# Eight DRAM-to-DRAM copies of 384-column bias lines in place of eight broadcast stores of 160-column pieces

## The chip, the core and the metric

The kernel runs on one core of one Trainium2 chip. The metric is the device time of one execution in microseconds (us); the time of a kernel is the median of its runs. A profiled execution gives in addition the span from its first to its last instruction, and what each engine, the queue of SP and the DMA engines did in it.

## The reference, cut to what matters

A decoder layer on 2048 tokens plus 16 meta tokens: RMSNorm, one input projection to 1952 columns, three token mixers side by side (latent attention with 6 heads, differential attention with 4 heads, sliding-window attention with 6 heads), an output projection, a SwiGLU feed forward, and a last norm. Heads of the second and third mixer add a relative position bias, which depends on the distance of query and key alone:

```
n = max(q_pos - k_pos, 0)
bucket = n if n < 16 else min(16 + int(log(n / 16) / log(128 / 16) * 16), 31)
logits = q . k * scale + rel_bias[bucket, head]      # 10 heads with a bias
```

All distances from 128 on share the last bucket. So a head's bias is one line over the distance, and a tile of 128 queries by some keys is that line, read one place further along from query to query.

## The kernel before, in words

The work has four phases on one core: phase A (norm, input projection, latent projections, all results to DRAM), phase B (full attention of latent and differential heads), the window attention with the output projection, and the feed forward.

**Phase A** (line 186) goes over 17 tiles of tokens, `t` = 0 to 16: tile 0 holds the meta tokens, the others 128 tokens each. A tile projects its tokens in four chunks of columns (`project`, matmuls at lines 122 to 124), splits the results into a high and a low half on ACT and DVE (`hilo`, lines 299 and 300), transposes them on PE (`flush`, line 346), copies the transposes out of PSUM (lines 350 and 352) and stores them to DRAM (lines 355 to 372). In the middle of tile `t` the tokens of tile `t + 1` are squared for the norm (ACT, line 325) and transposed (PE, line 332). The tokens themselves are loaded by line 213 into the two buffers of `xt`. The results for V go to a tile `vs` with one buffer, stored by line 475 to `vd`.

**The bias lines** are made beside this. `bias_lines` (line 257) is a generator; the loop of tiles advances it by one step in each tile from `t` = 4 on:

```
if t >= 4:
    next(lines, None)
```

A step loads a piece of a one-hot table (`hot`, line 271), multiplies it with the bias table on PE (line 273), copies the product to SBUF (line 275) and stores it into `ld` in DRAM (line 276) 128 times over, once for each partition, by a source that is repeated:

```
w = LINE // 4                                # 160 columns
...
nc.sync.dma_start(out=ld[r0:r0 + m, :, c:c + w],
                  in_=line[0:m, 0:w].unsqueeze(1).to_broadcast([m, P, w]))
```

There are 17 lines, 11 in the first group (`m` = 11) and 6 in the second, of `LINE` = 640 columns in four pieces each: eight steps, hence the tiles 4 to 11. `ld` is laid out `[17, 128, 640]`: line, partition, column. Each run that a store writes is 160 columns of 4 bytes long.

**Who reads `ld`.** `skew` (line 149) reads it with a step of one element less than a row from partition to partition, so that each partition gets the line one place further on. Phase B does it twice at its start (`ncaus`, lines 531 and 532), the window attention three times (`nswa`, lines 850 to 852).

**What sets the order.** All transfers are issued by SP, in one queue, in the order of a scheduler that works through the whole program with a timeline of its own. On each engine it places an instruction as soon as, on that timeline, what the instruction needs is there; so a load that needs nothing can stand far ahead of its place in the text of the program. What the scheduler has put in order is issued in that order.

Of the kernel before, what the change touches and what calls it, by code (L numbers as in the profile page):

```python
# [10 lines left out]
F32 = mybir.dt.float32  # L11
# [6 lines left out]
DRAM = bass.MemoryType.DRAM  # L18

P = 128  # L20
# [9 lines left out]
NB = 32  # L30
# [4 lines left out]
LINE = 640  # L35
# [12 lines left out]
# input projection: columns grouped as they are multiplied  # L48
# [7 lines left out]
# stacks, all [128, tokens] with high and low halves of float32 side by side  # L56
# [7 lines left out]
def constants():  # L64
    ident = np.eye(P, dtype=np.float32)
    fold = np.concatenate([np.eye(64), np.eye(64)]).astype(np.float32)
    inv = (10000.0 ** (-np.arange(0, 32, 2, dtype=np.float32) / np.float32(32))).astype(np.float32)
    pos = np.zeros((NT + 1, P), np.float32)
    pos[0, :META] = np.arange(META)
    pos[1:] = META + np.arange(SEQ).reshape(NT, P)  # L70
    ang = (pos[:, :, None] * inv).astype(np.float64)
    c, s = np.cos(ang), np.sin(ang)
    rope = np.concatenate([c, c, -s, s], -1).astype(np.float32).transpose(1, 0, 2)
    dist = 511 - np.arange(LINE)
    n = np.maximum(dist, 0)
    big = 16 + (np.log(np.maximum(n, 16) / 16.0) / math.log(DMAX / 16) * 16).astype(np.int64)
    bucket = np.where(n < 16, n, np.minimum(big, NB - 1))
    hot = np.zeros((2, NB + 1, LINE), np.float32)
    hot[:, bucket, np.arange(LINE)] = 1.0
    off = dist < 0  # L80
    far = off | (dist >= DMAX)
    for j, m in enumerate((off, far)):
        hot[j][:, m] = 0.0
        hot[j][NB, m] = 1.0
    return {"c_ident": ident, "c_fold": fold, "c_rope": np.ascontiguousarray(rope),
            "c_hot": np.ascontiguousarray(hot.transpose(1, 0, 2))}


def key_chunks(m):
    # 16 meta keys and m blocks of 128, in chunks of at most CH columns, and each in pieces of at most PW: (first column, width)  # L90
    out, c = [], 0
    for b in ([m] if m <= 8 else [-(-m // 2), m // 2]):
        w = b * P + (0 if c else META)
        n = -(-w // PW)
        pieces = []
        for j in range(n):
            k = (b // n + (1 if j >= n - b % n else 0)) * P + (0 if c else META)
            pieces.append((c, k))
            c += k
        out.append(pieces)  # L100
    return out
# [3 lines left out]
def trunk(ctx: ExitStack, tc: tile.TileContext, a, out):  # L105
# [13 lines left out]
    ld = dram.tile([NLINE, P, LINE], F32, name="ld")  # L119
# [9 lines left out]
    # ------------------------------------------------------------ constants  # L129
# [19 lines left out]
    def skew(dst, row, n, c0, w):  # L149
        # dst [P, n, w]: n lines, each one place further to the left from partition to partition  # L150
        src = bass.AP(tensor=ld.tensor, offset=ld.offset + row * P * LINE + 127 + c0, ap=[[LINE - 1, P], [P * LINE, n], [1, w]])
        nc.sync.dma_start(out=dst, in_=src)

    def merge_to(dst, x, y):
        # two lists of items side by side, in proportion to their costs
        tx, ty = sum(c for c, _ in x) or 1.0, sum(c for c, _ in y) or 1.0
        ix = iy = 0
        ax = ay = 0.0
        while ix < len(x) or iy < len(y):
            if iy >= len(y) or (ix < len(x) and ax / tx <= ay / ty):  # L160
                dst.append(x[ix])
                ax += x[ix][0]
                ix += 1
            else:
                dst.append(y[iy])
                ay += y[iy][0]
                iy += 1

    def rows_of(items):
        # items up to each one without cost, as one  # L170
# [14 lines left out]
    # ------------------------------------------------------------ phase A  # L185
    def phase_a():
        with ExitStack() as st:
            # the weights that the last tile needs first are at the edge, where phase B begins
# [68 lines left out]
            def bias_lines():  # L257
                # relative bias lines (negated, relative to the last bucket) and masks
# [7 lines left out]
                w = LINE // 4  # L266
                for j in range(2):
                    r0, m, b0 = ((0, 11, 0), (11, 6, 4))[j]
                    for c in range(0, LINE, w):
                        hot = stage.tile([P, SW], F32, name="raw")  # L270
                        nc.sync.dma_start(out=hot[0:NB + 1, 0:w], in_=a["c_hot"][:, j, c:c + w])
                        ps = psT.tile([P, 512], F32, name="psT")
                        nc.tensor.matmul(out=ps[0:m, 0:w], lhsT=rb[:, b0:b0 + m], rhs=hot[0:NB + 1, 0:w], start=True, stop=True)
                        line = stage.tile([P, SW], F32, name="raw")
                        nc.vector.tensor_copy(out=line[0:m, 0:w], in_=ps[0:m, 0:w])
                        nc.sync.dma_start(out=ld[r0:r0 + m, :, c:c + w], in_=line[0:m, 0:w].unsqueeze(1).to_broadcast([m, P, w]))
                        yield
# [24 lines left out]
            def rotate(dst, src, t, n):  # L302
                # src, dst: [P, n, 32]
# [36 lines left out]
            def flush(t, src, b, m):  # L340
                # transposed stacks b..b+m to DRAM
# [43 lines left out]
            for t in range(NT + 1):  # L385
# [10 lines left out]
                # [dk dv]  # L396
# [9 lines left out]
                # [c_kv k_rope sk sv]  # L406
# [23 lines left out]
                if not meta:  # L430
                    # [c_q dq]
# [10 lines left out]
                    # [sq]  # L442
# [10 lines left out]
                # latent projections  # L453
# [55 lines left out]
    # ------------------------------------------------------------ phase B  # L509
    def phase_b(window):  # L510
        with ExitStack() as st:
            # on the right what the last products with V no longer need
# [18 lines left out]
            skew(ncaus[:, 4:5, 256:], 10, 1, 256, 256)  # L531
            skew(ncaus[:, 0:4, 256:], 0, 4, 256, 256)
            # P^T of a pair's last key tile: the earlier query tile does not see it
# [6 lines left out]
            def softmax_row(items, i, mm_fn, cost, bias, fin):  # L540
                # items: the logits (negated) piece by piece of keys, with the maximum so far, then the row's
                # exponentials; fin(exponentials, row sum)
# [52 lines left out]
            def pv_pair(items, g, rows, v, fin):  # L595
                # O^T [high|low of v, 256 queries] of one head, then y = both halves, queries first
# [66 lines left out]
            def key_cols(q):  # L663
                # columns that the pairs 2q and 2q + 1 add
                return slice(0 if q == 0 else META + 512 * q, META + 512 * (q + 1))

            def order(h, last):
                # pairs of query tiles of a head; the last heads end with little
                return FORD if h == 0 else LORD if h == last else MORD

            def early(h, q):
                # only the first loads go ahead of the last stores of phase A
# [165 lines left out]
    # ------------------------------------------------------------ window attention, output projection  # L838
    def swa_setup(st):
# [10 lines left out]
        skew(nswa[:, 0, :, 0:16], 4, SH, 368, 16)  # L850
        skew(nswa[:, 0, :, 144:272], 11, SH, 384, 128)
        skew(nswa[:, 1, :, 16:272], 11, SH, 256, 256)
        return sw, sms, snk, nswa

    def phase_o(feed):
        with ExitStack() as st:
# [118 lines left out]
            # the half of w_out that is needed first  # L975
# [8 lines left out]
            # shared with the feed forward  # L984
            wk = shared.enter_context(tc.tile_pool(name="wk2", bufs=2, reuse_waits="tile"))
            common["wk"] = wk
            # what the last products no longer need is closed first
# [31 lines left out]
            def out_items(t):  # L1019
# [46 lines left out]
                def operands(r):  # L1066
                    # what this tile gives to the seven right operands of its chunk (see phase_f)
# [66 lines left out]
    # ------------------------------------------------------------ feed forward  # L1134
    def phase_f():
        # one level of Strassen's products: gate and up over halves of (features, d_model, tokens of a chunk),
        # down over halves of (tokens of a chunk, features, d_model)
        TH, FH = 512, NF // 2
        with ExitStack() as st:
# [16 lines left out]
            # gate and up, right operands: blocks x0, y0 (d_model halves of the first tokens) and x, y (of the second):  # L1156
            # x0 + y, x0, x - y, y0 - x0, y, x + x0, y0 + y
            # left operands: (first block, second block, sign); blocks are numbered 2 * feature half + d_model half
            WS = ((0, 3, 1), (2, 3, 1), (0, None, 1), (3, None, 1), (0, 1, 1), (2, 0, -1), (1, 3, -1))
            XORD = (0, 3, 4, 2, 6, 1, 5)  # L1160
            # down, left operands: blocks of h, numbered 2 * feature half + token half
            HS = ((0, 3, 1), (1, 3, 1), (0, None, 1), (3, None, 1), (0, 2, 1), (1, 0, -1), (2, 3, -1))
            # down, right operands: blocks of w_down, numbered 2 * feature half + column half
            DS = ((0, 3, 1), (0, None, 1), (1, 3, -1), (2, 0, -1), (3, None, 1), (0, 1, 1), (2, 3, 1))
            # (token half, column half, sign) of the sums that a product enters
# [4 lines left out]
            def gate_up():  # L1170
                with ExitStack() as s2:
                    # on the right what begins before the output projection has ended
# [9 lines left out]
                    def operand(c, i):  # L1182
                        # a right operand, split where it is
# [17 lines left out]
                    def weight(blk, i):  # L1201
                        # a left operand
# [21 lines left out]
                    def product(c, blk, close, after):  # L1224
                        # four blocks [128 features, 512 tokens], (feature half, token half), to close()
# [63 lines left out]
                    for n, (c, f, u) in enumerate(steps):  # L1289
# [5 lines left out]
                        def give(i):  # L1295
                            # what this block gives to the left operands of down
# [35 lines left out]
            def start_down():  # L1332
                # what begins before the last product of gate and up has ended
# [31 lines left out]
            def finish_down():  # L1365
                split_right, load_right, left, wsr, bwa, w0, x0 = (down[k] for k in ("split_right", "load_right", "left", "wsr", "bwa", "w0", "x0"))
                with ExitStack() as s2:
# [8 lines left out]
                    def raw(b, f):  # L1376
                        # a block of w_down; the blocks on the diagonal stay
# [57 lines left out]
                    def update(c, i, j, ps):  # L1435
                        # a finished product of token tile j of a half, into the sums
# [75 lines left out]
```

## Time and profile before

| | us |
|---|---|
| time, median of 3 runs | 2902.93 |
| time, lowest and highest | 2899.53, 2908.26 |
| span of the profiled execution | 2904.6 |
| PE busy in it | 2746.6 (95%) |
| DVE, ACT, POOL busy | 1795.9, 1447.5, 1318.6 |

The time of the profiled execution is not given apart from its span; the span lies among the three times. In the profile, PE is TensorE, PEld its weight loads, DVE, ACT and POOL are VectorE, ScalarE and GpSimd, SPq is the queue of SyncE, from which the transfers are issued. A duration on SPq is the time that one issue takes there, not that of its transfer. `PEclk` is the granted clock of TensorE as a share of its upper level of 2.4 GHz (0.50 is the lower level, 1.2 GHz), and `DMA share` the mean busy share of the core's 16 DMA engines. In a wait, the engine and line that waited stand left of the arrow and what it waited for stands right of it.

### The profile page before, as it was taken

The page shows a single profiled execution, that of the slowest core. Times are in us where ns is not written, and L with a number is a line of the kernel's source. Part 1 is how long each engine was busy: PE and PEld are TensorE (multiplying, and loading weights), DVE is VectorE, ACT ScalarE, POOL GpSimd, SP SyncE. Part 2 cuts the span into 40 slices and gives each one's busy share as a digit, 9 for nine tenths or more (in the row PEclk, how much of TensorE's full clock was granted, in tenths as well). Part 3 has the DMA queues.
Part 4 walks back from the last instruction along what each step waited for, and adds up shares of the span by engine and source line. Part 5 has one row for each costly group of instructions (what it writes and reads, how often), then busy time and mean ns, then how long its engine had stood idle before and what let it go on. Part 6 is the DMA issues. An engine that isn't in the chain of part 4 may idle for free.

```text
span 2904.6 us, 44635 instructions
## 1 busy us (share of the span) xinstructions
PE 2746.6 (95%) x14767; PEld 2357.7 (81%) x14767; DVE 1795.9 (62%) x4098; ACT 1447.5 (50%) x3264; POOL 1318.6 (45%) x1585
## 2 busy tenths in 40 slices
PE   7977779999999999989999899999999999999999
PEld 6866668888898999878888688888788888788887
DVE  6322223389898888855545866666866666565564
ACT  6433334478887888864443433334433334343343
POOL 1211112268788788831213555554655554232241
PEclk9988889999999999999999999999999999999999
DMA  7555444684556444366665633324423332944564
GB/s 195 140 125 122 108 113 138 170 236 110 148 120 157 109 122 98 83 196 185 191 184 184 211 106 109 105 89 163 141 95 109 109 98 89 322 133 135 169 194 145
DMA packets 427250, 417.80 MB, mean 144 GB/s; under 512 B 56415, under 2 KB 318202, under 8 KB 425226
## 3 DMA queue, kind: packets, MB, share of 16 engines
q1 hardware_dynamic: 427018, 414.94, 49.7%
q8 instruction: 117, 1.92, 0.3%
q14 instruction: 115, 0.94, 0.1%
HBM read 275.45 MB, written 139.39 MB: 143 GB/s over the span
## 4 chain that ended last, share of the span: by engine, by line
PE 79%; DMA 7%; DVE 4%; issue 4%; SPq 2%; ACT 2%; POOL 2%; POOLq 0%; ACTq 0%; DVEq 0%
PE ps L1221 9%; PE ps L1220 9%; PE ps L1219 9%; PE psO L638 5%; PE psTb L608 4%; PE ps L122 4%; PE ps L123 4%; PE ps L124 4%; PE psA L122 4%; PE psA L123 4%; PE psA L124 4%; PE psS L798 2%; PE psAo L122 2%; PE psAo L124 2%; PE psAo L123 2%
## 5 line engine op out<-in xcount | busy, mean ns | idle before, releaser
L1220 PE MATMUL ps<-x,wgh 128*128 128x512 f32 x1232 | 485.2, 394 | 6.2 <-DVE x L1189 6.1
L1221 PE MATMUL ps<-x,wgl 128*128 128x512 f32 x1232 | 484.9, 394 | 2.2 <-DVE wgl L1211 2.2
L1219 PE MATMUL ps<-x,wgh 128*128 128x512 f32 x1232 | 483.3, 393 | 3.8 <-ACT x L1188 3.8
L1151 POOL TENSOR_TENSOR wsum<-r 128x512 f32<-128x512 f32 x220 | 322.6, 1471 | 333.4 <-DVE wgl L1211 332.0
L575 ACT ACTIVATE p<-p,mn 128x656 f32<-128x656 f32 (+8 forms) x336 | 305.4, 915 | 32.4 <-DVE mn L570 31.4
L1210 ACT CAST wgh<-wsum 128x512 fp32r<-128x512 f32 x220 | 136.3, 620 | 313.8 <-PE ps L1220 205.8
L1220 PEld LDWEIGHTS ps<-x,wgh 128*128 128x128 f32 x1232 | 231.9, 188 | 63.4 <-DVE x L1189 10.7
L1219 PEld LDWEIGHTS ps<-x,wgh 128*128 128x128 f32 x1232 | 232.2, 188 | 57.8 <-ACT x L1188 5.3
L1221 PEld LDWEIGHTS ps<-x,wgl 128*128 128x128 f32 x1232 | 232.0, 188 | 53.7 <-DVE wgl L1211 2.6
L122 PE MATMUL ps<-bh,wgh 128*128 128x512 f32 x616 | 241.5, 395 | 3.2 <-ACT wgh L1356 3.2
L123 PE MATMUL ps<-bl,wgh 128*128 128x512 f32 x616 | 243.2, 395 | 0.0
L124 PE MATMUL ps<-bh,wgl 128*128 128x512 f32 x616 | 238.3, 393 | 0.0
L1211 DVE TENSOR_TENSOR wgl<-wsum,wgh 128x512 fp32r<-128x512 f32 x220 | 189.7, 863 | 58.8 <-ACT wgh L1210 57.8
L608 PE MATMUL psTb<-ident,p 128*128 128x128 f32 x1440 | 218.6, 277 | 2.8 <-DVE ptl L620 1.4
L122 PE MATMUL psA<-wi,xh 128*128 128x512 f32 (+2 forms) x528 | 207.9, 394 | 6.0 <-ACT wi L237 4.8
L123 PE MATMUL psA<-wi,xh 128*128 128x512 f32 (+2 forms) x528 | 202.6, 384 | 0.3 <-DVE wi L238 0.3
L1356 ACT CAST wgh<-wgl 128x512 fp32r<-128x512 f32 x154 | 95.0, 620 | 214.4 <-DMA wgl<-fd 170.1
L124 PE MATMUL psA<-wi,xl 128*128 128x512 f32 (+2 forms) x528 | 201.0, 381 | 0.0
L1357 DVE TENSOR_TENSOR wgl<-wgl,wgh 128x512 fp32r<-128x512 f32 x154 | 117.8, 774 | 131.3 <-ACT wgh L1356 124.8
L638 PE MATMUL psO<-pth,vt 128*128 128x256 f32 x720 | 192.6, 288 | 2.3 <-ACT p L575 2.0
L638 PE MATMUL psO<-ptl,vt 128*128 128x256 f32 x720 | 192.9, 296 | 0.8 <-DVE ptl L620 0.2
L1151 POOL TENSOR_TENSOR hs<-c 128x512 f32<-128x512 f32 x108 | 157.1, 1461 | 55.1 <-DVE c L1310 49.0
(255 smaller groups left out, 6862.7 us busy)
## 6 DMA issues: line engine op xcount, KB each, us to landing
wgl<-fd SPq DMA_DIRECT2D x154, 256.0 KB
fd<-hs SPq DMA_DIRECT2D x110, 256.0 KB
qm<-qd SPq DMA_DIRECT2D x92, 256.0 KB
r<-in_w_gate_dram SPq DMA_DIRECT2D x88, 256.0 KB
r<-in_w_up_dram SPq DMA_DIRECT2D x88, 256.0 KB
ws<-in_w_down_dram SPq DMA_DIRECT2D x77, 256.0 KB
qd<-so SPq DMA_DIRECT2D x80, 192.0 KB
qf<-qd SPq DMA_DIRECT2D x60, 256.0 KB
```

The costliest lines, as they stand in the source:

```text
L122: nc.tensor.matmul(out=ps, lhsT=xh, rhs=wh, start=start, stop=False)
L123: nc.tensor.matmul(out=ps, lhsT=xh, rhs=wl, start=False, stop=False)
L124: nc.tensor.matmul(out=ps, lhsT=xl, rhs=wh, start=False, stop=stop)
L575: nc.scalar.activation(out=x[:, 0:m], in_=x[:, 0:m], func=AF.Exp, bias=mn[:, n:n + 1], scale=-1.0, accum_out=rsum[:, k:k + 1])
L608: nc.tensor.transpose(pt[:, j * 256 + q * P:j * 256 + (q + 1) * P], cols(rows[q], c), ident)
L638: nc.tensor.matmul(out=ot[:, 0:256], lhsT=v[:, vb], rhs=x, start=(st_["n"] == 1), stop=(st_["n"] == 2 * total))
L1151: eng.tensor_tensor(out=out, in0=x, in1=y, op=ALU.add if sign > 0 else ALU.subtract)
L1210: nc.scalar.copy(out=h, in_=src)
L1211: nc.vector.tensor_tensor(out=l, in0=src, in1=f32(h), op=ALU.subtract)
L1219: nc.tensor.matmul(out=ps, lhsT=h[:, k], rhs=o[:, 0, k], start=k == 0, stop=False)
L1220: nc.tensor.matmul(out=ps, lhsT=h[:, k], rhs=o[:, 1, k], start=False, stop=False)
L1221: nc.tensor.matmul(out=ps, lhsT=l[:, k], rhs=o[:, 0, k], start=False, stop=k == 3)
```

## The change

Lines have 384 columns instead of 640 (distances 255 to -128 instead of 511 to -128; the skewed reads start 256 columns earlier, so that they read the same values). A group's line is made in one step, of 384 columns, and stored once, into a small DRAM tile `l1` `[17, 384]`. Eight further steps copy `l1` to `ld`, which is now laid out `[128, 17, 384]`: each copies all 17 lines, 26,112 bytes in one piece, for 16 partitions. The generator so has ten steps instead of eight: two that make lines and eight that copy, in the tiles 4 to 13. The diff, without edits of comments:

```
-LINE = 640
+LINE = 384
...
-    dist = 511 - np.arange(LINE)
+    dist = 255 - np.arange(LINE)
...
-    ld = dram.tile([NLINE, P, LINE], F32, name="ld")
+    l1 = dram.tile([NLINE, LINE], F32, name="l1")
+    ld = dram.tile([P, NLINE, LINE], F32, name="ld")
...
     def skew(dst, row, n, c0, w):
-        src = bass.AP(tensor=ld.tensor, offset=ld.offset + row * P * LINE + 127 + c0, ap=[[LINE - 1, P], [P * LINE, n], [1, w]])
+        src = bass.AP(tensor=ld.tensor, offset=ld.offset + row * LINE + 127 + c0, ap=[[NLINE * LINE - 1, P], [LINE, n], [1, w]])
...
-                w = LINE // 4
                 for j in range(2):
                     r0, m, b0 = ((0, 11, 0), (11, 6, 4))[j]
-                    for c in range(0, LINE, w):
-                        hot = stage.tile([P, SW], F32, name="raw")
-                        nc.sync.dma_start(out=hot[0:NB + 1, 0:w], in_=a["c_hot"][:, j, c:c + w])
-                        ps = psT.tile([P, 512], F32, name="psT")
-                        nc.tensor.matmul(out=ps[0:m, 0:w], lhsT=rb[:, b0:b0 + m], rhs=hot[0:NB + 1, 0:w], start=True, stop=True)
-                        line = stage.tile([P, SW], F32, name="raw")
-                        nc.vector.tensor_copy(out=line[0:m, 0:w], in_=ps[0:m, 0:w])
-                        nc.sync.dma_start(out=ld[r0:r0 + m, :, c:c + w], in_=line[0:m, 0:w].unsqueeze(1).to_broadcast([m, P, w]))
-                        yield
+                    hot = stage.tile([P, SW], F32, name="raw")
+                    nc.sync.dma_start(out=hot[0:NB + 1, 0:LINE], in_=a["c_hot"][:, j])
+                    ps = psT.tile([P, 512], F32, name="psT")
+                    nc.tensor.matmul(out=ps[0:m, 0:LINE], lhsT=rb[:, b0:b0 + m], rhs=hot[0:NB + 1, 0:LINE], start=True, stop=True)
+                    line = stage.tile([P, SW], F32, name="raw")
+                    nc.vector.tensor_copy(out=line[0:m, 0:LINE], in_=ps[0:m, 0:LINE])
+                    nc.sync.dma_start(out=l1[r0:r0 + m], in_=line[0:m, 0:LINE])
+                    yield
+
+                for b in range(0, P, 16):
+                    nc.sync.dma_start(out=ld[b:b + 16].rearrange("p n c -> p (n c)"),
+                                      in_=l1.rearrange("(o n) c -> o (n c)", o=1).to_broadcast([16, NLINE * LINE]))
+                    yield
...
-            skew(ncaus[:, 4:5, 256:], 10, 1, 256, 256)
-            skew(ncaus[:, 0:4, 256:], 0, 4, 256, 256)
+            skew(ncaus[:, 4:5, 256:], 10, 1, 0, 256)
+            skew(ncaus[:, 0:4, 256:], 0, 4, 0, 256)
...
-        skew(nswa[:, 0, :, 0:16], 4, SH, 368, 16)
-        skew(nswa[:, 0, :, 144:272], 11, SH, 384, 128)
-        skew(nswa[:, 1, :, 16:272], 11, SH, 256, 256)
+        skew(nswa[:, 0, :, 0:16], 4, SH, 112, 16)
+        skew(nswa[:, 0, :, 144:272], 11, SH, 128, 128)
+        skew(nswa[:, 1, :, 16:272], 11, SH, 0, 256)
```

## Rows read from the trace of the kernel before

**Rows 1.** The page: TensorE's granted clock in 40 equal slices of the span.

```profile
PEclk9988889999999999999999999999999999999999
```

**Rows 2.** Chain that ended last: start us, us, what; the transposes that bound tiles.

```profile
55.88 0.90 PE psT L332 x8
...
141.34 0.90 PE psT L332 x8
...
452.86 0.87 PE psT L332 x8
...
536.69 0.87 PE psT L332 x8
```

**Rows 3.** Busy time by stretch of phase A: three tiles, eight tiles, three tiles.

```profile
core 0: us, PE busy (x) PEld busy (x) DVE busy (x) ACT busy (x) POOL busy (x), PEclk, DMA share, GB/s
55.90:141.30 85.40, 84.34 (x498) 75.89 (x497) 31.99 (x75) 39.18 (x111) 18.56 (x50) 1.00 0.51 141
141.30:452.90 311.60, 240.81 (x1303) 213.88 (x1302) 88.60 (x204) 101.45 (x284) 47.06 (x129) 0.86 0.50 117
452.90:536.70 83.80, 82.21 (x487) 74.03 (x486) 31.39 (x73) 37.36 (x105) 17.30 (x48) 1.00 0.47 131
```

**Rows 4.** PE's wait in 141.3 to 452.9: total us, times, longest us.

```profile
PE psT L346 <- DVE gm L300: 68.9, 12, 10.1
```

**Rows 5.** ACT's wait for tokens, in 141.3 to 452.9, then in 452.9 to 536.7.

```profile
ACT sq L325 <- DMA xt<-in_x_dram: 102.8, 8, 14.5
...
ACT sq L325 <- DMA xt<-in_x_dram: 0.9, 2, 0.5
```

**Rows 6.** SP's queue in a tile of the first three: start us, us, issue.

```profile
113.34 0.43 SPq L368 DMA_DIRECT2D wd<-so  x1
113.82 0.46 SPq L372 DMA_DIRECT2D wd<-so  x1
114.71 0.35 SPq L213 DMA_DIRECT2D xt<-in_x_dram  x1
```

**Rows 7.** SP's queue in the tile after it, with a step of the lines.

```profile
138.57 0.96 SPq L276 DMA_DIRECT2D ld<-raw  x1
139.57 4.15 SPq L271 DMA_DIRECT2D raw<-in_c_hot_dram  x1
144.16 2.91 SPq L359 DMA_DIRECT2D kd<-so  x1
147.13 3.27 SPq L368 DMA_DIRECT2D wd<-so  x1
150.46 3.02 SPq L372 DMA_DIRECT2D wd<-so  x1
153.59 0.54 SPq L213 DMA_DIRECT2D xt<-in_x_dram  x1
```

**Rows 8.** Busy time by stretch behind a store of 11 lines, then of 6.

```profile
142.00:150.00 8.00, 8.00 (x47) 6.96 (x46) 2.59 (x5) 2.51 (x6) 0.00 (x0) 1.00 0.61 77
...
299.00:307.00 8.00, 8.00 (x45) 6.96 (x44) 2.63 (x6) 2.34 (x6) 0.00 (x0) 1.00 0.33 49
```

**Rows 9.** Busy time by stretch inside the tile that begins at 141.3.

```profile
155.00:160.00 5.00, 0.00 (x0) 0.00 (x0) 0.00 (x0) 1.03 (x2) 0.00 (x0) 0.79 0.77 208
160.00:165.00 5.00, 2.94 (x14) 2.62 (x14) 3.50 (x10) 3.91 (x14) 0.73 (x2) 0.50 0.39 107
```

**Rows 10.** ACT in a tile of the first three; idle before it, and for what, in brackets.

```profile
118.37 1.06 ACT L325 ACTIVATE sq<-xt 128x1024 bf16<-128x1024 f32 x1 [0.60 <-DMA xt<-in_x_dram]
...
122.86 0.48 ACT L352 COPY so<-psT 128x384 f32<-128x384 f32 x1 [3.03 <-PE psT L346]
...
133.04 0.47 ACT L299 ACTIVATE vs<-psA,rs 128x256 fp32r<-128x256 f32 x1 [4.83 <-DMA vd<-vs]
```

**Rows 11.** Chain that ended last: the two passes of a line's matmul.

```profile
137.09 0.37 PE psT L273 x2
```

**Rows 12.** SP's queue near the start: a load that `bias_lines` issues.

```profile
14.60 0.42 SPq L263 DMA_DIRECT2D rb<-in_rel_bias_dram  x1
```

**Rows 13.** Busy time of the stretch with the highest DMA rate looked at, in the feed forward.

```profile
2500.00:2520.00 20.00, 16.77 (x65) 12.90 (x64) 12.04 (x17) 5.50 (x9) 4.16 (x3) 0.91 1.04 396
```

**Rows 14.** Instructions on the skewed tile of phase B: ns min/median/max, first and last start us.

```profile
L570 DVE CUSTOM_DVE_ANT_0 p<-psS,ncaus x42: 297/434/575, 578.7 to 1137.6; 128x400 f32<-128x400 f32 x14, 128x144 f32<-128x144 f32 x14, 128x272 f32<-128x272 f32 x14
...
L152 SPq DMA_DIRECT2D ncaus<-ld x2: 448/458/467, 538.2 to 538.7; - x2
```

## The prediction

> **What bounds the kernel now.** I read the page first. Its row of the granted clock is full but for slices 2 to 5, some 145 to 436 us [rows 1]; that is phase A, and the steps of the bias lines run there. Next the chain that ended last: it passes through the token transposes of every tile, so their starts bound the tiles [rows 2]. Then busy time by stretch between those edges [rows 3]. Three tiles before the steps take 85.4 us and three after them 83.8, so a tile without a step takes 169.2 / 6 = 28.2 us, with PE busy for 166.55 / 6 = 27.76 of it and the clock at 1.00. The eight tiles behind a step take 311.6 us, 38.95 each. PE is idle for 311.6 - 240.8 = 70.8 us of that, and its busy time is 240.8 instead of 8 x 27.76 = 222.1.
>
> The waits say why. PE's idle time is its wait for the halves that ACT and DVE make [rows 4], and ACT, which works in order, had been standing at the squares of the next tokens: 102.8 us in eight waits for their load, against 0.9 in two waits in the three tiles after the steps [rows 5]. The load is late because it is issued late. In a tile without a step SP issues `wd`, `wd` and the tokens at under half a microsecond each [rows 6]; behind the store to `ld` the one-hot load, `kd` and the two `wd` take 2.9 to 4.2 us each, and the tokens go out 153.59 - 138.57 = 15.0 us behind that store [rows 7]. All of these small transfers stand behind the store in one queue. In the eight microseconds behind a store of 11 lines the DMA engines are busy at 0.61 and move 77 GB/s; behind one of 6 lines, 0.33 and 49 GB/s [rows 8]. The first store is 11 x 128 x 640 B = 901 KB, 11.7 us at 77 GB/s; the second is 492 KB, 10.0 us at 49 GB/s. A store of nearly half the bytes thus holds the queue almost as long. A shape in which each line keeps one DMA engine busy explains it: 11/16 = 0.69 and 6/16 = 0.38, near the shares.
>
> The Trainium skill states such a rule (DMA: Bandwidth & Descriptors, Why a DMA increments its semaphore by 16 and not by 1): a copy runs on the largest number of engines up to 16 that divides the outermost counts on both sides. The shares of [rows 8] agree; by it a copy with 16 outermost would have 16 engines.
>
> The gap is paid twice. After PE's idle 155 to 160 us the granted clock is 0.50, 1.2 GHz, in the next 5 us [rows 9]; this is most of the 240.8 - 222.1 = 18.7 us by which PE is busy longer.
>
> **The change, part by part.**
>
> *Eight broadcast stores go.* With them go the late tokens, ACT's stand, PE's idle time and the lower clock behind it: 311.6 - 8 x 28.2 = **-86.0 us**. What is late next in such a tile is seen in the six without a step: nothing; PE is busy for 27.76 of 28.2 us, so PE's own work is the next bound.
>
> *Two lines of 384 columns instead of eight pieces of 160.* The two passes of a piece take 0.37 us on PE [rows 11]; of 384 columns 0.37 x 384 / 160 = 0.89. The eight old ones are already inside the 311.6 us, the six reference tiles hold none, so two new ones on a PE that is full cost **+1.8 us**. The two PSUM copies and two stores to `l1` (17 rows of 1,536 B, 26 KB together) lie beside PE's work; DVE is busy for 32 of 85 us [rows 3].
>
> *Eight copies of 16 x 26,112 B = 417.8 KB.* The trace has no DRAM-to-DRAM transfer, so I bound one from both sides. Below: at the highest rate looked at, 396 GB/s [rows 13], 417.8 KB take 1.06 us. Above: at the rate of one engine in the slowest store, 77 / 11 = 7.0 GB/s [rows 8], one engine's 26,112 B take 3.7 us. Long runs on all engines speak for the low end, a read and a write of DRAM at once and one source for all engines for the high end; I take 2.0 us, the geometric middle. No gain is possible here; the copies are added work.
>
> The same page (Latency and other measured facts) gives 207 GB/s for copies between HBM tensors, and 103 where rows lie a large power of two apart, which speaks against such copies; estimates from it are 2.0 and 4.1 us a copy. With 4.1 us and all eight ahead of the tokens the sum below would end some 3 us above its upper bound. No run here shows it yet.
>
> *Where they are issued.* In the program the copies stand one per tile, in the tiles 6 to 13. But a copy needs nothing except the two stores to `l1`, and the scheduler does not hold back what needs nothing: the load of the bias table, which `bias_lines` issues in tile 4, was issued at 14.6 us [rows 12]. So I expect most of the eight right behind the second store to `l1`, in one burst in tiles 5 and 6, at some 165 to 185 us. The first copy adds a wait on SP for that store to land. Behind it in the queue stand `kd`, `wd`, `wd` and the tokens, and ACT's squares wait for the tokens.
>
> A burst occupies all engines for 8 x 1.06 = 8.5 to 8 x 3.7 = 30 us. What covers it: ACT stands idle 3.03 us behind the squares anyway [rows 10], and the engines are idle for half of a tile, 14 us (share 0.51 [rows 3]). Lower end: every copy falls behind the tokens and into idle engine time, 0 us. Upper end: all eight are ahead of the tokens, 30 - 3 = 27 us, and some 4 us for a PE at the lower clock: 31. I take half of them ahead of the tokens: 4 x 2.0 = 8, less 3 of cover, and 1 for the clock: **+6 us**. Were this cover gone, the tokens would be late by the whole 8. The store of `vs` comes next: ACT waits 4.83 us for it in a tile without a step, and PE does not stop [rows 10], so it has some slack too.
>
> *The skewed reads* keep number, bytes and length of runs; only the steps between runs differ. Those of phase B are issued 40 us before their first use [rows 14], and a burst of copies ends some 250 us ahead of them: 0, with both bounds inside that cover. Those of the window attention come after the whole of phase B and are taken as unchanged.
>
> The sum is 2904.6 - 86.0 + 1.8 + 6 = 2826.4 on the span of the profiled execution. That span is 1.7 us above the median of the runs, so I forecast **2825 us**. The bounds of the burst make it 2819 to 2850.
>
> **The rivals.**
>
> *One copy per tile.* If the copies stay in their tiles, each delays the tokens by at most 3.7 us against 3 of cover, 8 x 0 to 8 x 0.7: 2819 to 2825. For it: the stores went out at their places; against: they had to wait for a product of their tile, and the copies have none. The time is hardly another, but the picture is.
>
> *Copies far dearer than the nearest rows.* Sixteen engines read the same 26 KB at the same moment, and no row shows what this does. At twice the upper bound, 7.4 us, the burst is 59 us and all of it shows but the cover, 3: 2904.6 - 86.0 + 1.8 + 60 = 2880, or 2879 against the median. Still faster.
>
> *A copy that runs on one engine* (the other side). If the lowering puts the whole repeated source on one ring, that engine moves 417.8 KB a copy. At 396 / 16 = 24.8 GB/s this is 16.8 us, 135 for eight, and every transfer with a share on that ring waits: 2904.6 - 86.0 + 1.8 + 135 - 3 = 2952, less 1.7: about 2951. It decides from 84 + 3 = 87 us for all eight, 11 us a copy. Against it stands that 11 and 6 outermost lines kept about that many engines busy [rows 8], so 16 should keep 16.
>
> *Late tokens in every tile with a step, whatever it moves.* Then ten steps instead of eight stall, 86.0 / 8 = 10.75 us each: 2903 + 21.5 = 2924. Against it: 901 KB and 492 KB moved the stall little, but by the same runs per engine, which a copy does not have. If only a part of the mechanism holds, the result could also land at no change.
>
> **How the numbers follow.** My forecast with a burst, within 2819 to 2850, has 0.62; one copy per tile 0.20; dearer copies 0.10; one engine 0.03; stalls in every step 0.03; no change 0.02. The first two lie within 2819 to 2850. Between runs the kernel varies by 4 us either way, and if the tiles go like the last three (27.9 us) 2 us more are gained; so the range is 2812 to 2852, which holds 0.80 with what may be off in the first two. A difference of about 0.3%, 9 us, is what a measurement of this kernel can tell from none: faster by more 0.92, the same 0.02, slower 0.06.
>
> **What would show it.** In the changed profile all tiles of phase A take 27 to 29 us, but perhaps one or two at the burst; ACT's wait for the tokens falls from 102.8 us to under 20; the granted clock stands at 9 in slices 2 to 5; the issues of `kd` and `wd` take under half a microsecond in most tiles; the copies follow the second store to `l1` closely. I am wrong if the tokens stay late in many tiles, if DMA share is near 1/16 for tens of microseconds behind a copy, or if phase A ends later than some 470 us where the last tile edge read was at 536.7 [rows 2].

## The result, and the profile after

The changed kernel takes 2811.7 us, the median of four runs (2810.05 to 2814.4), against 2903.27 for the kernel before (four runs; the three in the table ahead of the prediction gave 2902.93). The ratio is 0.9684, with a 95% interval of 0.967 to 0.9698: 91.6 us less. The forecast was 2825 with a range of 2812 to 2852, so the time came out faster, as forecast, and 0.3 us below the lower end.

The page of the changed kernel first: the span, PE's busy time, and the granted clock in 40 slices.

```profile
span 2808.3 us, 44596 instructions
...
PE 2724.7 (97%) x14755; PEld 2339.2 (83%) x14755; DVE 1794.5 (64%) x4092; ACT 1450.3 (52%) x3264; POOL 1309.9 (47%) x1585
...
PEclk9999999899999999899999999999999999999999
```

The four slices below 9 in phase A, the third to the sixth [rows 1], are gone; the two that stand at 8 now lie behind it. Next, busy time by stretch in the changed kernel, between the same tile edges as [rows 3]: three tiles, the eight that used to follow a store, three tiles.

```profile
55.40:141.10 85.70, 84.64 (x498) 75.84 (x497) 32.26 (x76) 39.17 (x111) 18.47 (x50) 1.00 0.51 141
141.10:363.80 222.70, 218.93 (x1291) 196.32 (x1290) 85.35 (x198) 102.39 (x284) 47.10 (x129) 1.00 0.54 154
363.80:447.60 83.80, 82.21 (x488) 74.03 (x487) 31.41 (x73) 37.35 (x105) 17.41 (x48) 1.00 0.47 131
```

The eight tiles take 222.7 us instead of 311.6, PE is busy in 218.9 of them, and the clock stands at 1.00 throughout. The tiles around them take what they took before. In the same eight tiles the waits of ACT for the tokens and of PE for the halves, 102.8 and 68.9 us before [rows 4, 5], are now these (total us, times, longest):

```profile
ACT sq L329 <- DMA xt<-in_x_dram: 7.2, 8, 2.4
...
PE psT L350 <- DVE gm L304: 2.9, 3, 1.0
```

SP's queue in the changed kernel shows where the copies went (start us, us of issue; `l` is `l1`).

```profile
167.07 0.41 SPq L275 DMA_DIRECT2D l<-raw  x1
169.51 1.21 SPq L279 DMA_DIRECT2D ld<-l  x2
170.81 0.53 SPq L363 DMA_DIRECT2D kd<-so  x1
171.40 0.42 SPq L372 DMA_DIRECT2D wd<-so  x1
171.87 0.49 SPq L376 DMA_DIRECT2D wd<-so  x1
172.46 0.41 SPq L214 DMA_DIRECT2D xt<-in_x_dram  x1
172.91 1.11 SPq L279 DMA_DIRECT2D ld<-l  x2
174.12 0.53 SPq L359 DMA_DIRECT2D qd<-so  x1
174.78 2.36 SPq L279 DMA_DIRECT2D ld<-l  x4
```

All eight were issued within 8 us, right behind the second store to `l1`: two ahead of the tokens, six behind. `kd`, `wd` and `wd` are issued in half a microsecond each, where they took 2.9 to 3.3 us behind a broadcast store [rows 7]. The tile of the burst, between its neighbours, again as busy time by stretch, and ACT's squares in it, with the wait in brackets:

```profile
141.10:170.10 29.00, 28.38 (x167) 24.96 (x166) 11.53 (x26) 12.59 (x35) 6.10 (x17) 1.00 0.47 134
170.10:197.00 26.90, 26.81 (x161) 24.10 (x160) 10.94 (x25) 13.16 (x36) 5.61 (x16) 1.00 0.90 268
197.00:225.70 28.70, 27.72 (x166) 25.02 (x165) 10.37 (x24) 12.87 (x36) 6.20 (x17) 1.00 0.47 134
...
177.09 1.06 ACT L329 ACTIVATE sq<-xt 128x1024 bf16<-128x1024 f32 x1 [2.36 <-DMA xt<-in_x_dram]
```

The tokens are 2.36 us late, less than the 3.03 us that ACT stands idle behind the squares anyway [rows 10], and PE is busy for 26.81 of 26.9 us: the burst costs nothing. Its price can be estimated from the DMA share. 0.90 of 26.9 us is 24.2 us of all engines; the neighbours' 0.47 would be 12.6. The difference, 11.6 us, is the eight copies: some 1.45 us each. The trace also holds a record of every single packet, with its size and duration. In it the 128 packets of 26,112 bytes take 0.97 to 2.11 us, 1.40 on average; sixteen at a time, this is 1.4 us a copy, or 417.8 KB / 1.4 us = 298 GB/s. The page's packet counts of the two kernels show how long their pieces are (before, then after):

```profile
DMA packets 427250, 417.80 MB, mean 144 GB/s; under 512 B 56415, under 2 KB 318202, under 8 KB 425226
```

```profile
DMA packets 418504, 415.53 MB, mean 148 GB/s; under 512 B 56426, under 2 KB 309328, under 8 KB 416352
```

Packets of 8 KB and more rise from 427250 - 425226 = 2024 to 418504 - 416352 = 2152. The 128 more are 8 x 16: each partition's 26,112 bytes went as one packet.

### The profile page after: what moved, and what is told of

It is laid out like the page before. It is cut to its first block, busy times and chain, and to the rows that moved or that the text cites. A ratio compares the mean times of both kernels' runs of the same rounds, so it can differ in the third digit from the quotient of the medians.

```text
span 2808.3 us, 44596 instructions
## 1 busy us (share of the span) xinstructions
PE 2724.7 (97%) x14755; PEld 2339.2 (83%) x14755; DVE 1794.5 (64%) x4092; ACT 1450.3 (52%) x3264; POOL 1309.9 (47%) x1585
## 2 busy tenths in 40 slices
DMA packets 418504, 415.53 MB, mean 148 GB/s; under 512 B 56426, under 2 KB 309328, under 8 KB 416352
## 4 chain that ended last, share of the span: by engine, by line
PE 81%; DMA 6%; DVE 4%; issue 4%; POOL 2%; ACT 2%; SPq 1%; POOLq 0%; DVEq 0%; ACTq 0%
PE ps L1225 10%; PE ps L1224 10%; PE ps L1223 10%; PE psO L642 5%; PE psA L123 4%; PE psTb L612 4%; PE psA L125 4%; PE psA L124 4%; PE ps L125 4%; PE ps L123 4%; PE ps L124 4%; PE psAo L123 2%; PE psAo L125 2%; PE psAo L124 2%; PE psS L802 2%
## 5 line engine op out<-in xcount | busy, mean ns | idle before, releaser
L123 PE MATMUL psA<-wi,xh 128*128 128x512 f32 (+2 forms) x528 | 203.4, 385 | 5.5 <-ACT wi L238 4.7
L124 PE MATMUL psA<-wi,xh 128*128 128x512 f32 (+2 forms) x528 | 199.7, 378 | 0.4 <-DVE wi L239 0.3
```

Source lines behind the costliest of these rows:

```text
L123: nc.tensor.matmul(out=ps, lhsT=xh, rhs=wh, start=start, stop=False)
L124: nc.tensor.matmul(out=ps, lhsT=xh, rhs=wl, start=False, stop=False)
```

## The experiments

The gain lies in phase A, as forecast. What the traces alone do not settle: whether it is the place of the stores or the transfers themselves that cost; whether 384 columns or the copies bring the gain; what a copy costs when there are more than the idle time covers; and whether the number of engines follows the outermost count.

**One: the old stores, moved behind the tokens.** In the kernel before, a step leaves its store for later, and it is issued behind the next load of tokens:

```
-                        nc.sync.dma_start(out=ld[r0:r0 + m, :, c:c + w], in_=line[0:m, 0:w].unsqueeze(1).to_broadcast([m, P, w]))
+                        common.setdefault("st", []).append(lambda r0=r0, m=m, c=c, line=line: nc.sync.dma_start(out=ld[r0:r0 + m, :, c:c + w], in_=line[0:m, 0:w].unsqueeze(1).to_broadcast([m, P, w])))
...
+                if t >= 6 and common["st"]:
+                    with tc.issue_after(common["xt"]):
+                        common["st"].pop(0)()
```

> The kernel before with all its eight broadcast stores, each issued right behind the next tokens' load instead of ahead of it. Theory: the stall comes of the store standing ahead of the tokens in SP's queue. Then ACT's wait for the tokens falls from 102.8 us to under 20, the eight tiles take 28 to 33 us instead of 38.95, and the time is 2815 to 2860 us; what is left of the stall is another transfer that the store now holds up (qd or vd). Rival: the transfers as such cost the time, by the engines or the bandwidth they take, wherever they stand. Then the tiles stay near 39 us and the time near 2903.

Measured: 2891.96 us, ratio 0.9955 (0.9938 to 0.9972). The tokens are hardly late any more, yet most of the stall stays: the eight tiles take 298.2 us, 37.3 each. ACT's waits from 140 to 450 us in this kernel, and SP's queue behind one moved store:

```profile
ACT so L352 <- DMA qd<-so: 53.2, 7, 8.4
...
ACT sq L325 <- DMA xt<-in_x_dram: 13.8, 9, 2.6
```

```profile
142.67 0.40 SPq L213 DMA_DIRECT2D xt<-in_x_dram  x1
143.13 0.94 SPq L276 DMA_DIRECT2D ld<-raw  x1
144.34 12.31 SPq L355 DMA_DIRECT2D qd<-so  x3
```

ACT's wait for the tokens fell to 13.8 us, as the first theory had it; in its place ACT waits 53.2 us for the three buffers of `so`, whose stores to `qd` now stand behind the broadcast store. SP spends 12.31 us on three issues of `qd`. Neither theory holds whole: the place decides which engine waits for what, but a queue held for 12 us found something to stall at both places tried. 13 us is what the better place is worth, 92 what the whole change is.

**Two: the copies in the stores' place.** In the changed kernel each copy is held behind the `kd` store of its own tile, so that it stands where a broadcast store had stood:

```
                 for b in range(0, P, 16):
-                    nc.sync.dma_start(out=ld[b:b + 16].rearrange("p n c -> p (n c)"),
-                                      in_=l1.rearrange("(o n) c -> o (n c)", o=1).to_broadcast([16, NLINE * LINE]))
+                    with tc.issue_after(common["kd"]):
+                        nc.sync.dma_start(out=ld[b:b + 16].rearrange("p n c -> p (n c)"),
+                                          in_=l1.rearrange("(o n) c -> o (n c)", o=1).to_broadcast([16, NLINE * LINE]))
```

> The changed kernel with its eight copies held back to one per tile, each in the very place in SP's queue that a broadcast store had (behind kd, ahead of kd, wd, wd and the tokens). Theory: place costs nothing when the transfer is short; each copy delays the tokens by 1 to 3.7 us and ACT has 3 us to spare, so tiles take 27 to 29 us and the time is 2808 to 2820 us, the same as the changed kernel's 2811.7. Rival: the changed kernel gains because the copies are moved out of their tiles into one burst; then tiles with a copy stall and the time is 2840 to 2903.

Measured: 2807.59 us, ratio 0.9676 (0.965 to 0.9701), not to be told from the changed kernel, and 0.4 us below the range expected. SP's queue at the first copy, and busy time by stretch over the eight tiles with copies:

```profile
194.01 0.58 SPq L280 DMA_DIRECT2D ld<-l  x1
195.25 0.34 SPq L364 DMA_DIRECT2D kd<-so  x1
195.64 0.46 SPq L373 DMA_DIRECT2D wd<-so  x1
196.15 0.54 SPq L377 DMA_DIRECT2D wd<-so  x1
196.97 0.34 SPq L214 DMA_DIRECT2D xt<-in_x_dram  x1
```

```profile
196.10:418.40 222.30, 218.27 (x1290) 196.39 (x1289) 83.79 (x196) 102.27 (x284) 47.31 (x129) 1.00 0.55 154
```

Same place, same number, another transfer: 222.3 / 8 = 27.8 us a tile instead of 38.95. So the burst is not what brings the gain, and one copy per tile hides as well as eight in a row.

**Three: 384 columns without copies.** In the kernel before, the lines have 384 columns, made in two steps, but each group is still stored by one broadcast store:

```
-LINE = 640
+LINE = 384
...
-                w = LINE // 4
+                w = LINE
```

with the table and the skewed reads as in the change.

> The kernel before with lines of 384 columns made in two steps, as in the change, but still stored by a broadcast store each: 128 runs of 1536 bytes on 11 and on 6 engines, no copies. If an engine is held by the number of runs (128 as before, 10 to 12 us), two stalls of 10.75 us are left: 2811.7 + 21.5 = 2833. If by bytes (7 to 8 GB/s, 25 to 28 us each), two stalls of 25 to 29 us: 2862 to 2870.

Measured: 2868.3 us, ratio 0.9874 (0.9859 to 0.9889), the upper of the two forecasts. Busy time by stretch of the two tiles behind the two stores, and of the stretches in which the stores run:

```profile
140.60:197.80 57.20, 31.69 (x167) 27.77 (x166) 11.54 (x26) 12.40 (x35) 6.09 (x17) 0.73 0.56 106
197.80:251.90 54.10, 29.19 (x161) 26.16 (x160) 11.05 (x25) 12.96 (x36) 5.55 (x16) 0.75 0.42 92
...
140.00:160.00 20.00, 12.36 (x76) 10.88 (x74) 3.70 (x7) 2.67 (x6) 0.71 (x1) 0.86 0.64 80
197.00:215.00 18.00, 12.28 (x75) 10.81 (x73) 3.19 (x6) 2.86 (x6) 0.70 (x1) 0.93 0.39 61
```

Two tiles of 57.2 and 54.1 us cost 111.3 - 2 x 27.8 = 55.7 us. At 1536 bytes a run the stores still move 80 and 61 GB/s, little more than the 77 and 49 of 640-byte runs [rows 8]: the hold goes with the bytes, not with the count of 128 runs. So fewer columns alone bring 2905.01 (the runs of before taken beside it) - 2868.3 = 36.7 us, less than half of the change's 92.

The rest comes with the copies, and they differ from the stores in three things at once: all 16 engines, pieces of 26 KB, and DRAM as their source instead of 11 or 6 partitions of SBUF. No run parts all three. The length of the pieces is the least likely of them. By the packet records one engine moves 7.5 and 7.9 GB/s in the 1536-byte pieces here, 7.7 and 8.5 in the 640-byte pieces of the kernel before, but 17.6 in the 512-byte pieces that phase A stores from all 128 partitions. Whether the few source partitions are what slows a store was not tried; in all these stores one line is one partition and one engine.

**Four: four times the copies.**

```
-                    nc.sync.dma_start(out=ld[b:b + 16].rearrange("p n c -> p (n c)"),
+                    for q in range(4):
+                        nc.sync.dma_start(out=(ld, *more)[q][b:b + 16].rearrange("p n c -> p (n c)"),
```

> The changed kernel with each copy made four times, into four tensors: 32 copies instead of 8. At 1.06 us a copy the 24 more take 25 us of all engines, which the idle half of two tiles covers: 2811 to 2820. At 2.0 us they take 48 us, of which some 20 show: 2830. At 3.7 us they take 89 us and some 55 show: 2865.

Measured: 2843.57 us, ratio 0.9786 (0.9771 to 0.9801). The 24 additional copies cost 31.9 us over the changed kernel, 1.3 each. The packet records of this run give 1.29 us of engine time a copy, near the 1.40 of the burst above, so of the additional ones little is hidden on balance, as if the first eight had used up the cover. The price of a copy that I had put at 2.0 us is thus 1.3 to 1.4, and the cover is smaller than this expectation assumed, which had 2811 to 2820 for 1.06 us a copy and 2830 for 2.0. Busy time by stretch where the burst of 32 bites, and the wait in which it shows:

```profile
205.00:210.00 5.00, 0.00 (x0) 0.00 (x0) 0.42 (x1) 0.25 (x1) 0.00 (x0) 0.89 0.90 274
210.00:215.00 5.00, 0.00 (x0) 0.00 (x0) 0.00 (x0) 0.00 (x0) 0.00 (x0) 0.50 1.06 363
```

```profile
ACT so L358 <- DMA kd<-so: 11.1, 1, 11.1
```

The engines are full (shares of 0.90 and 1.06) at 274 and 363 GB/s, PE is idle, and ACT waits again for a buffer of `so`, as in the first experiment.

**Five: copies on one engine.** The copies take 17 partitions each, seven times, and 9 at the end:

```
-                for b in range(0, P, 16):
+                for b in range(0, P, 17):
+                    k = min(17, P - b)
```

> The changed kernel with its copies cut for 17 partitions each (seven of 17 and one of 9) instead of 16; 17 has no divisor up to 16 but 1. If a copy runs on as many engines as divide its outermost count, seven copies of 444 KB each run on one engine, 18 us each at 24.8 GB/s, 125 us in all, with 15 to 20 us of cover: 2910 to 2950 us, slower than the kernel before, with a DMA share of little over 1/16 for long stretches. If the copies are spread over all engines whatever the count: 2808 to 2816.

Measured: 2913.34 us, ratio 1.0043 (1.0029 to 1.0057): one partition more per copy turns the gain of 92 us into a loss of 13. Busy time by stretch, one entry of SP's queue, and ACT's longest wait:

```profile
190.00:210.00 20.00, 0.00 (x0) 0.00 (x0) 1.21 (x3) 2.36 (x7) 0.73 (x2) 0.50 0.11 40
210.00:230.00 20.00, 3.16 (x15) 2.77 (x15) 1.71 (x6) 1.29 (x5) 0.00 (x0) 0.50 0.06 26
```

```profile
205.13 32.98 SPq L280 DMA_DIRECT2D ld<-l  x4
```

```profile
ACT so L357 <- DMA qd<-so: 79.9, 3, 48.9
```

A DMA share of 0.06 is one engine of sixteen, at 26 GB/s. SP needs 33 us to issue four copies, and the small transfers stand behind them. This is the rival of the forecast in which a copy runs on one engine. By the rule of the Trainium skill that the prediction cites (DMA: Bandwidth & Descriptors, Why a DMA increments its semaphore by 16 and not by 1) an outermost count of 17 gets one engine and a count of 16 gets sixteen. The traces agree: the share is 0.06 with 17 here, and 0.83 with 16 rows in the next experiment.

**Six: stores of 16 rows.** Both groups of lines are filled up to 16 rows, so that the old stores run on 16 engines:

```
-    ld = dram.tile([NLINE, P, LINE], F32, name="ld")
+    ld = dram.tile([32, P, LINE], F32, name="ld")
...
-                    r0, m, b0 = ((0, 11, 0), (11, 6, 4))[j]
+                    r0, m, b0 = ((0, 16, 0), (16, 16, 4))[j]
```

> The kernel before with both groups of lines filled up to 16 rows (the added rows are zeros and are not read): all eight stores are of 16 x 128 runs of 640 bytes, 1.31 MB, 45 to 167 per cent more bytes than before. If each row holds one engine with 128 runs, and the engines don't share another limit, an engine is held as long as before: DMA share 0.85 to 0.95 behind a store, tiles of 39 us, 2895 to 2915 us. If the bytes of a store set the hold at 75 GB/s, 17.5 us each: 2940 to 2970.

Measured: 2909.27 us, ratio 1.003 (1.0021 to 1.004). Busy time by stretch behind two of the stores, to be set beside [rows 8]:

```profile
142.00:150.00 8.00, 8.00 (x45) 6.88 (x44) 2.92 (x6) 1.93 (x5) 0.00 (x0) 1.00 0.83 96
...
299.00:307.00 8.00, 8.00 (x47) 6.96 (x45) 2.59 (x5) 2.53 (x6) 0.00 (x0) 1.00 0.84 94
```

The share is 0.83 where 11 rows had 0.61 and 6 rows 0.33, just under the 0.85 expected. 45 to 167 per cent more bytes cost 9 us over the runs of before that were taken beside it (2900.36), so it is not the bytes of a store that set the hold but the bytes per engine, which here are also the bytes per source partition. An engine is a little slower beside more others: by the packet records a 640-byte piece takes some 76 ns beside five other engines, 84 beside ten and 90 beside fifteen, which is 8.5, 7.7 and 7.1 GB/s an engine.

**Seven and eight: the two kernels again,** for the stretches behind phase A.

> The kernel before, profiled a second time, for the stretches behind phase A. Phase A should end at 537 us as before. If the 7.8 us that the changed kernel is shorter in the stretch from the first use of the window attention's bias tile to the first product of the feed forward (354.0 against 346.2 us) come of the change, this stretch is 352 to 356 us again; if it varies from run to run, it may be anywhere from 346 to 359.

> The changed kernel, profiled a second time, for the same stretch. Phase A should end at 448 us. If the shorter stretch is the change's, it is 344 to 348 us again; if it varies from run to run, anywhere from 346 to 359.

Measured: 2900.36 and 2813.08 us. The table gives, in us, the last token transpose's start (end of phase A), from there to the first use of `nswa` in the window attention, from there to the first product of the feed forward, and the rest of the span:

| profile | end of A | to window attention | to feed forward | rest | span |
|---|---|---|---|---|---|
| before | 537.3 | 695.9 | 354.0 | 1317.4 | 2904.6 |
| before again | 538.2 | 694.6 | 350.2 | 1315.6 | 2898.6 |
| after | 448.2 | 698.0 | 346.2 | 1315.9 | 2808.3 |
| after again | 449.2 | 700.3 | 346.7 | 1315.1 | 2811.3 |

Phase A ends 89.1 and 89.0 us earlier in the two pairs. Behind it the four profiles take 2367.3, 2360.4, 2360.1 and 2362.1 us. Only the first stands apart, and it is the one that the forecast was summed on. The stretch to the feed forward varies by 4 us in the kernel before and stays some 4 us shorter in the changed one; the stretch ahead of it is 2 to 6 us longer. Whether these two small differences are the change's own, by the altered order of instructions, was not tried; together they come to nothing.

## Why the prediction came out as it did

*The bound.* Right. ACT stood at the squares for tokens held in the queue behind a broadcast store, PE idled and came back at the lower clock; without the stores all of it is gone. But the tokens were only the first to meet the held queue: with the tokens ahead of the store (experiment one) 13 us were gained and no more.

*-86.0 us for the stall.* Right, and a little short. The eight tiles went from 311.6 to 222.7 us, 88.9 less, with the second line's matmul already in them. The reference of 28.2 us a tile was too high, because its six tiles are not like the eight. In the changed kernel the eight take 28.7 to 29.1 and 26.8 to 27.1 us by turns, 27.84 on average. Of the six, only one is plainly of the short kind, and the first is the longest of all. Both as busy time by stretch, from the kernel before:

```profile
55.90:85.00 29.10, 29.01 (x173) 26.31 (x172) 11.20 (x26) 13.65 (x40) 6.46 (x18) 1.00 0.54 145
...
481.70:508.40 26.70, 26.70 (x160) 23.99 (x159) 10.46 (x25) 12.64 (x35) 5.54 (x16) 1.00 0.51 143
```

PE is busy for 29.01 us of the first: it has more work there, and does not wait. The third of the six, from 113.8 us, holds the first of the eight old pieces, at 137.09 us [rows 11]; the prediction has all eight in the 311.6 us and none in the six.

*+1.8 us for the lines.* A little too much. The two passes of 384 columns take 0.74 us in the chain, not 0.89, so 1.5 for both, and one of the two lines again falls into the tile ahead of the eight.

*Where the copies are issued.* Right: one burst right behind the second store to `l1`, at 169.5 to 177 us, read from a load that had been issued 120 us ahead of its place [rows 12].

*+6 us for the burst.* **This is the step that failed; it measured 0.** The form was right, copies ahead of the tokens times their price, less ACT's 3 us. Both factors were too high: two copies stood ahead of the tokens and not four, and a copy takes 1.4 us and not 2.0. 2 x 1.4 = 2.8 lies inside the 3.0 of cover. I had taken the geometric middle between the fastest load and the slowest store; the trace puts it near the fast end. A nearer price stood in [rows 3]: 141 GB/s at a share of 0.51 is 276 GB/s with all engines busy, by which a copy would take 1.5 us. The Trainium skill gives 207 GB/s for copies between HBM tensors whose rows lie 512 KiB apart (DMA: Bandwidth & Descriptors, Latency and other measured facts). The copies here, with rows 26,112 bytes apart, ran at 298 GB/s, so the estimate of 2.0 us from that figure was too high as well.

*The range.* Phase A came out 89.1 us shorter in the profiles, the sum had 78.2: 6 us of the difference are the burst, 5 the tiles with their lines. Some 2.5 us more lie between phase A's gain and the medians' 91.6; runs of one kernel differ by that much. The lower end of the range had the burst at 0 already (2819), and took off 4 us for the runs and 2 for the tiles. With the burst at 0 the sum has phase A 84.2 us shorter; it came out 89.1 us shorter, so the tiles with their lines gave 4.9 us more where 2 were allowed, and the 2 us that remain are within what runs differ by. So it is the size of the tile that put the time 0.3 us below the range, while of the 13 us between forecast and time the burst is the largest part and the tile the second.

*The rivals.* One copy per tile gives the same time (experiment two). Copies far dearer than the nearest rows: refuted, 1.4 us a copy. One engine: the mechanism is real and ends slower than before (experiment five), but 16 partitions avoid it. Late tokens in every tile with a step: refuted, 7.2 us of waiting in eight tiles.

## What to carry to other kernels

A transfer is priced by the bytes that its busiest DMA engine has to move and by the rate of that engine: 7 to 8.5 GB/s here for lines read again and again out of a few SBUF partitions, 18.7 for the copies out of DRAM. It costs not only its own wait but everything issued behind it in the queue. Look at the DMA share behind it: a share that stands at 0.06, 0.33 or 0.61 for microseconds while SP's small issues grow from 0.4 to 3 us says that a few engines hold the queue. Make the outermost count a multiple of 16 and the bytes fewer before looking for a better place in the order; the place alone was worth 13 of 92 us here. Longer runs by themselves, 1536 bytes instead of 640, did not raise the rate of an engine.

## What the runs showed of the hardware that was not expected

- Sixteen engines that read the same 26 KB of DRAM at once and write 16 places move 298 GB/s: a packet takes 1.40 us on average, 18.7 GB/s an engine. On one engine alone (experiment five) the same packet takes 0.97 us in the median, 27 GB/s. Whether the common source or the other engines' work makes the difference was not tried.
- Runs of 1536 bytes from 11 SBUF partitions are hardly faster than runs of 640 bytes (80 against 77 GB/s for 11 engines), while 512-byte runs from 128 partitions move 17.6 GB/s an engine, more than twice as much. That the few source partitions are the limit would fit, but was not tried.
- Moving a long store behind the transfer that waited for it helped by only 13 us: the wait passed from the tokens to the buffers of the next stores.
